# A final norm by token: rows turned first, squares summed along the row on ScalarE

## The chip, the cores and the metric

The kernel runs on one core of a Trainium2 chip. The metric is the device time of one execution in microseconds (us), the median of several runs. Engines: TensorE (PE) multiplies matrices, VectorE (DVE) and ScalarE (ACT) work on tiles of 128 partitions, GpSimd (POOL) is nearly idle here, SyncE (SP) issues DMAs, and so does ACT.

## The reference

One decoder layer on 512 tokens of 1024 features, fp32: a SwiGLU FFN, a mixer, a second FFN, then a gated embedding and a final norm. The last two are what the change touches:

```
gate = jax.nn.sigmoid(rmsnorm(h, ple_norm[i]) @ ple_w_gate[i] + ple_b_gate[i])
h = h + gate * (p[i] @ ple_w_proj[i])
return rmsnorm(h, final_norm)

def rmsnorm(x, g):
    y = xf * lax.rsqrt(jnp.mean(xf * xf, axis=-1, keepdims=True) + EPS)
    return (y * g.astype(jnp.float32)).astype(x.dtype)
```

## The kernel before, in words

Activations lie feature by feature: h[0] to h[7] are tiles of 128 features (partitions) by 512 tokens. In the program's names h[0], h[1], h[2], h[3] are h_91, h_92, h_93, h_94, and h[4] to h[7] are h_97, h_95, h_96, h_98. A product with a weight tile is done in three passes of split numbers (whi, wlo by x), 8 times over: 24 matmuls into one PSUM bank (b). The kernel first records all its operations; then it issues them in the order of ORDER, a table of unit numbers written out by hand or by a planner, engine queues being filled in that order. Each engine then runs its own queue strictly in order.

The last stage starts where the weights of ple_gate come in: raw (loaded by SP), whi (a cast on ACT), wlo (a subtraction on DVE). The token factors of the norm before it come from column sums, a root by Newton steps on DVE, a spread matmul, and a copy to rall on ACT. Then for each of the 8 feature tiles gate() multiplies the product by rall on DVE, takes the sigmoid with the bias on ACT, multiplies by the embedding and adds to h on DVE. For d = 0 to 4 this is done for all 512 tokens at once; the last three (BY_HALF = 3) are done by halves of 256 tokens: first the three for the first half, then the three for the second.

The final norm of before works by feature up to the end. gate() squares the new h (ACT, the last tile on DVE), the squares of the first five tiles are added into one tile (total, in the trace ssum), gained() multiplies h by the norm's vector, feature by feature. factors() sums over the partitions with matmuls against a column of ones (128x1), in fp32, for two chunks of 128 tokens, and takes the root by ACT's Sqrt table (rsqrt_by_table). rows_out() then turns h (4 transposes of 128 x 128 make one bank of 128 tokens by 512 features), and an evacuation multiplies by the token's factor and writes o, which goes to DRAM. The turns of both halves stand behind the last product.

Of the kernel before, what the change touches and what calls it, by code (L numbers as in the profile page):

```python
# [29 lines left out]
P = 128  # L30
# [22 lines left out]
    "m": 33, "convin": 2, "o": 8, "sq": 4,  # L53
}
REGION = dict.fromkeys(("raw0", "s0", "embt", "F", "xfa", "xfb", "x", "xa", "xb", "r4", "u", "emb"), "left") | dict.fromkeys(
    ("rawb", "whix", "wlox", "s1", "rawd", "ghi", "glo", "g", "u2", "p7", "m", "convin", "o", "sq"), "right",
# [20 lines left out]
for _name, _w in _VECS:  # L77
# [211 lines left out]
def layer_kernel(ctx: ExitStack, tc: tile.TileContext, a: dict, out: bass.AP):  # L289
# [1508 lines left out]
    def gate(d, ps, tok, engine):  # L1798

        t = tmp()[:, tok]  # L1800
        nc.vector.tensor_tensor(t, ps[:, tok], r[:, tok], ALU.mult)
        nc.scalar.activation(t, t, AF.Sigmoid, bias=col("ple_b_gate", d))
        engine.tensor_tensor(t, t, emb[d][:, tok], ALU.mult)
        engine.tensor_tensor(h[d][:, tok], h[d][:, tok], t, ALU.add)
        sq = tmp() if tok is whole else sb("sq", (P, half))
        if d < ND - 1:
            nc.scalar.activation(sq, h[d][:, tok], AF.Square)
        else:
            nc.vector.tensor_tensor(sq, h[d][:, tok], h[d][:, tok], ALU.mult)
        return sq  # L1810

    def gained(d, tok):

        if d < ND - 1:
            nc.scalar.activation(h[d][:, tok], h[d][:, tok], AF.Copy, scale=col("final_norm", d))
        else:
            nc.vector.tensor_scalar(
                h[d][:, tok], h[d][:, tok], col("final_norm", d), None, ALU.mult
            )

    total = sb("ssum")

    def done(d, ps):
        sq = gate(d, ps, whole, nc.vector)
        if d == 0:
            nc.vector.tensor_copy(total, sq)
        else:
            nc.vector.tensor_tensor(total, total, sq, ALU.add)
        gained(d, whole)

    for d in range(ND - BY_HALF):
        ps = mm_ps()
        accumulate(ps, weights(a["ple_gate"][d], D), 0, x)
        if d == 0:
            tok, first = norm.per_token(D), ps
            continue
        if d == 1:
            r = Norm.on_all(tok)
            done(0, first)
        done(d, ps)  # L1840
    units = [weights(a["ple_gate"][d], D) for d in range(ND - BY_HALF, ND)]
    def gate_half(i, tok):
        d = ND - BY_HALF + i
        ps = sm_ps()
        accumulate(ps[:, tok], units[i], 0, x, tokens=tok)
        sq = gate(d, ps, tok, nc.vector)
        gained(d, tok)
        return sq

    def factors(tok, sqs):  # L1850

        chunks = range(tok.start // P, tok.stop // P)
        ps = sm_ps()
# [8 lines left out]
        return rt  # L1862

    def rows_out(tok, rt):
        for i, c in enumerate(range(tok.start // P, tok.stop // P)):
            for q in range(2):
                ps = mm_ps()
                for d in range(4):
# [144 lines left out]
```

## Time and profile before

| | |
|---|---|
| median of 3 runs | 1074.15 us (1074.07 to 1074.2) |
| the profiled execution | 1073.36 us |
| its span, from first to last instruction | 1071.6 us |
| busy: PE, DVE, ACT, POOL | 99%, 76%, 52%, 7% of the span |
| granted TensorE clock | 0.999 of full |
| DMA | 173.27 MB, mean 162 GB/s |

Times in the rows are us from the span's start, durations us unless marked ns. A row of the timeline that stands for several instructions gives the time from the first's start to the last's end. PEld is the loading of the stationary tile, beside PE. A queue's name with a q (SPq, ACTq) is the issue of DMAs.

### The profile page before, as it was taken

The numbers are of one execution on the slowest core, as the hardware profiler recorded it, in microseconds if no ns is written. First come the engines' busy times: TensorE is split into PE (matmuls) and PEld (weight loads), VectorE is DVE, ScalarE is ACT, GpSimd is POOL, SyncE is SP. The second block draws the span as 40 slices with busy tenths as digits, with TensorE's granted clock in tenths as the row PEclk, the third lists the DMA queues.
The fourth block names the chain that finished last, engine by engine and source line by source line (L and its number), as shares of the span: only waits on it lengthen the run. The fifth ranks groups of instructions, "written<-read, shape, count | busy, mean of one in ns | idle before, by whom it ended". The sixth has DMA issues, their size and how long they took to land.

```text
span 1071.6 us, 17611 instructions
## 1 busy us (share of the span) xinstructions
PE 1062.1 (99%) x7151; PEld 965.0 (90%) x7151; DVE 817.0 (76%) x1169; ACT 559.5 (52%) x781; POOL 75.2 (7%) x95
## 2 busy tenths in 40 slices
PE   9999999999999999999999999999999999999997
PEld 7899999999998878998999888999999999999887
DVE  6978685867577879999999767988667575857866
ACT  7655344444444537887865435654434343534545
POOL 1100000100000000000100000010100000000000
PEclk9999999999999999999999999999999999999999
DMA  9876765766452236777855435786755757633412
GB/s 322 238 202 166 196 181 193 196 181 174 99 154 82 65 113 146 187 201 175 212 135 130 138 98 137 218 236 186 204 143 155 211 144 197 181 115 85 139 53 79
DMA packets 52209, 173.27 MB, mean 162 GB/s; under 512 B 5920, under 2 KB 6176, under 8 KB 52128
## 3 DMA queue, kind: packets, MB, share of 16 engines
q1 hardware_dynamic: 33696, 116.93, 32.1%
q0 software_dynamic: 12256, 44.57, 23.1%
q10 hardware_dynamic: 6176, 10.65, 3.4%
q8 instruction: 56, 0.92, 0.3%
q14 instruction: 25, 0.20, 0.1%
HBM read 167.86 MB, written 4.26 MB: 161 GB/s over the span
## 4 chain that ended last, share of the span: by engine, by line
PE 99%; DVE 0%; ACT 0%; issue 0%; DVEq 0%; ACTq 0%
PE b L1905 81%; PE a L1905 18%; DVEq L2008 0%; DVE o L1905 0%; ACT m L1905 0%; ACT b L1905 0%; DVE tmp L1905 0%; DVE h L1905 0%; DVE ones L410 0%; DVE nv L1905 0%; ACTq L1905 0%
## 5 line engine op out<-in xcount | busy, mean ns | idle before, releaser
L1905 PE MATMUL b<-xfb,whi 128*128 128x256 f32 (+1 forms) x1704 | 297.5, 278 | 0.7 <-ACT b L1905 0.7
L1905 PEld LDWEIGHTS b<-xfb,whi 128*128 128x128 f32 x1704 | 261.0, 188 | 6.0 <-ACT b L1905 0.9
L1905 PE MATMUL b<-xfb,wlo 128*128 128x256 f32 (+1 forms) x852 | 237.2, 278 | 0.0
L1905 ACT CAST whi<-raw 128x1024 fp32r<-128x1024 f32 (+1 forms) x131 | 136.0, 1041 | 146.4 <-PE b L1905 109.7
L1905 DVE TENSOR_TENSOR wlo<-raw,whi 128x1024 fp32r<-128x1024 f32 (+1 forms) x130 | 156.8, 1212 | 28.7 <-ACT whi L1905 25.8
L1905 PEld LDWEIGHTS b<-xfb,wlo 128*128 128x128 f32 x852 | 159.9, 188 | 0.5
L1905 PE MATMUL b<-xfa,whi 128*128 128x256 f32 (+1 forms) x696 | 124.0, 281 | 0.0
L1905 PEld LDWEIGHTS b<-xfa,whi 128*128 128x128 f32 x696 | 107.0, 188 | 2.5 <-DVE xfa L1905 0.2
L1905 PE MATMUL b<-xfa,wlo 128*128 128x256 f32 (+1 forms) x348 | 97.8, 281 | 0.0
L1905 ACT CAST whix<-rawd 128x1024 fp32r<-128x1024 f32 (+1 forms) x40 | 39.4, 986 | 88.5 <-PE a L1905 47.9
L1905 DVE TENSOR_TENSOR wlo<-rawb,whi 128x1024 fp32r<-128x1024 f32 x51 | 62.1, 1220 | 23.2 <-ACT whi L1905 23.1
L1905 ACT CAST whi<-rawb 128x1024 fp32r<-128x1024 f32 x51 | 53.3, 1049 | 48.8 <-PE b L1905 39.7
L1905 PE MATMUL b<-m,whi 128*128 128x512 f32 x224 | 69.6, 392 | 0.0
L1905 DVE TENSOR_TENSOR wlox<-rawd,whix 128x1024 fp32r<-128x1024 f32 (+1 forms) x40 | 45.7, 1143 | 27.0 <-ACT whix L1905 26.9
L1905 PEld LDWEIGHTS b<-xfa,wlo 128*128 128x128 f32 x348 | 65.4, 188 | 0.5
L1905 PE MATMUL b<-xb,whi 128*128 128x256 f32 (+1 forms) x280 | 62.2, 318 | 0.0
L1905 PE MATMUL b<-ghi,wlox 128*128 128x512 f32 x156 | 61.4, 394 | 0.0
L1905 PE MATMUL b<-glo,whix 128*128 128x512 f32 x156 | 61.2, 392 | 0.0
L1905 PE MATMUL b<-ghi,whix 128*128 128x512 f32 x156 | 60.7, 389 | 0.0
L1905 PE MATMUL a<-ghi,wlox 128*128 128x512 f32 x140 | 55.2, 394 | 0.0
L1905 PE MATMUL a<-glo,whix 128*128 128x512 f32 x140 | 54.9, 392 | 0.0
L1905 PE MATMUL a<-ghi,whix 128*128 128x512 f32 x140 | 54.4, 389 | 0.0
(294 smaller groups left out, 2223.8 us busy)
## 6 DMA issues: line engine op xcount, KB each, us to landing
raw<-in_ffn_gu SPq DMA_DIRECT2D x57, 512.0 KB, 5.4
rawd<-in_ffn_down SPq DMA_DIRECT2D x40, 512.0 KB, 4.4
raw<-in_ffn_gu POOLq DMA_DIRECT2D x32, 512.0 KB, 7.7
rawb<-in_ffn_gu SPq DMA_DIRECT2D x31, 512.0 KB, 6.1
s<-in_ffn_gu SPq DMA_DIRECT2D x21, 512.0 KB, 5.5
s<-in_ffn_gu POOLq DMA_DIRECT2D x21, 512.0 KB, 8.5
raw<-in_w_out SPq DMA_DIRECT2D x16, 512.0 KB, 3.6
raw<-in_w_in SPq DMA_DIRECT2D x13, 512.0 KB, 3.7
```

The lines of the kernel that those rows point to most:

```text
L1905: getattr(getattr(real, engine), what)(*(real_of(x) for x in args), **{k: real_of(x) for k, x in kw.items()})
```

## The change

The norm is done by token on turned rows. As soon as h is final for four feature tiles and two chunks of tokens, these are turned into PSUM, and ACT squares them there and sums along the row in the same instruction (accum_out), in three parts for each half: all of the first four feature tiles, then three of the others, then the last one. The norm's vector is loaded once, spread to all partitions (fn, 512 KB, issued on ACT's queue), and multiplied in on the turned rows: for the first half together with the token's factor in one DVE instruction; for the second half the upper four features are multiplied by fn early (upper()) and by the factor on ACT. The first half takes its root by Newton steps on DVE (rsqrt), the second by the Sqrt table, which a small ACTIVATE calls in ahead. The column sums, the squares by feature, their total and gained() go. ORDER was written anew for this; the sizes of the other tiles' places were kept.

```diff
-    "m": 33, "convin": 2, "o": 8, "sq": 4,
+    "m": 33, "convin": 2, "o": 8, "ssq": 10, "fn": 1, "t": 6, "junk": 2,
...
-    "1-2 5-7 9-10 13 12 11 3 14 16 18 20 24 15 17 19 0 25 21 77 26 41 27 29 42 38 37 39-40 34 8 35 43 33 "
+    "1-2 5 0 6-7 9-10 13 12 11 3 14 16 18 20 24 15 17 19 25 21 77 26 41 27 29 42 38 37 39-40 34 8 35 43 "
...
-        engine.tensor_tensor(t, t, emb[d][:, tok], ALU.mult)
-        engine.tensor_tensor(h[d][:, tok], h[d][:, tok], t, ALU.add)
-        sq = tmp() if tok is whole else sb("sq", (P, half))
...
+        nc.vector.tensor_tensor(t, t, emb[d][:, tok], ALU.mult)
+        nc.vector.tensor_tensor(h[d][:, tok], h[d][:, tok], t, ALU.add)
+
+    fn = sb("fn", (P, D))
+    nc.scalar.dma_start(fn, a["fn"].partition_broadcast(P))
...
+        def turn(self, q, part=slice(0, 4)):
+            for i, c in enumerate(self.chunks):
...
+                for d in range(part.start, part.stop):
+                    nc.tensor.transpose(chunk(ps, d), chunk(h[4 * q + d], c), ident)
+
+        def squares(self, q, part, n):
+            for i in range(2):
+                w = slice(part.start * P, part.stop * P)
+                nc.scalar.activation(
+                    sb("junk")[:, w], self.ps[q, i][:, w], AF.Square, accum_out=self.ss[n][:, i : i + 1]
+                )
+
+        def upper(self):
+            for i in range(2):
+                self.o[0, i] = sb("o")
+                nc.vector.tensor_tensor(self.o[0, i], self.ps[0, i], fn[:, :T], ALU.mult)
...
+            for i, c in enumerate(self.chunks):
+                rows = out[c * P : (c + 1) * P]
+                if self.half:
+                    o = self.o[0, i]
+                    nc.scalar.activation(o, o, AF.Copy, scale=rt[:, i : i + 1])
+                else:
+                    o = sb("o")
+                    nc.vector.scalar_tensor_tensor(
+                        o, self.ps[0, i], rt[:, i : i + 1], fn[:, :T], ALU.mult, ALU.mult
+                    )
+                (nc.scalar if self.half else nc.sync).dma_start(rows[:, :T], o)
+                o = sb("o")
+                nc.vector.scalar_tensor_tensor(o, self.ps[1, i], rt[:, i : i + 1], fn[:, T:], ALU.mult, ALU.mult)
+                nc.sync.dma_start(rows[:, T:], o)
...
+    rows = [Rows(i) for i in range(2)]
+    for row in rows:
+        row.turn(0)
+        row.squares(0, slice(0, 4), 0)
+        if row.half:
+            row.upper()
...
+    for tok, row in zip(halves, rows):
+        for i in range(BY_HALF - 1):
+            gate_half(i, tok)
+        row.turn(1, slice(0, 3))
+        row.squares(1, slice(0, 3), 1)
+        row.so_far()
+        gate_half(BY_HALF - 1, tok)
+        if row.half:
+            nc.scalar.activation(sb("ssq", (P, 2)), ones[:, 0:2], AF.Sqrt)
+        row.turn(1, slice(3, 4))
+        row.squares(1, slice(3, 4), 2)
+        row.out()
```

First place: PE's queue behind the last half product (of h_98, second half). Before, the column sums (ones) follow it, and then the first of 32 turns (ident), of which the rest stand behind these.

```order
L1905 MATMUL b_10793<-x_10224,wlo_10691 128x256
L1905 MATMUL b_10854<-ones_71,ssum_10670 128x1 x2
L1905 MATMUL b_10854<-ones_71,sq_10395 128x1 x2
L1905 MATMUL b_10854<-ones_71,sq_10397 128x1 x2
L1905 MATMUL b_10854<-ones_71,sq_10398 128x1 x2
L1905 MATMUL b_10878<-ident_65,h_91 128x128
L1905 MATMUL b_10878<-ident_65,h_92 128x128
L1905 MATMUL b_10878<-ident_65,h_94 128x128
L1905 MATMUL b_10878<-ident_65,h_93 128x128
```

In the changed kernel the same product (now b_10834) is followed by eight turns alone, which end PE's queue.

```order
L1928 MATMUL b_10834<-x_10230,wlo_10643 128x256
L1928 MATMUL b_10895<-ident_65,h_97 128x128
L1928 MATMUL b_10895<-ident_65,h_95 128x128
L1928 MATMUL b_10895<-ident_65,h_96 128x128
L1928 MATMUL b_10899<-ident_65,h_97 128x128
L1928 MATMUL b_10899<-ident_65,h_95 128x128
L1928 MATMUL b_10899<-ident_65,h_96 128x128
L1928 MATMUL b_10895<-ident_65,h_98 128x128
L1928 MATMUL b_10899<-ident_65,h_98 128x128
```

The other 24 turns moved ahead: 8 stand before the product b_10777, the last but one, and 16 (banks b_10814, b_10819, b_10824, b_10829) between it and b_10834.

Second place: ACT's queue at the same time. Before, sigmoids (tmp), squares by feature (sq) and multiplications by the norm's vector (h) stand in turn, and the table load for the root follows the last sigmoid.

```order
L1905 ACTIVATE sq_10397<-h_96 128x256
L1905 ACTIVATE tmp_10835<-tmp_10835,vec_63 128x256
L1905 ACTIVATE h_95<-h_95,vec_63 128x256
L1905 ACTIVATE h_96<-h_96,vec_63 128x256
L1905 ACTIVATE tmp_10852<-tmp_10852,vec_63 128x256
L1905 ACTIVATE h_93<-h_93,vec_63 128x512
L1905 ACT_TABLE_LOAD
L1905 ACTIVATE ny_10872<-nv_10866 128x2
```

Now squares of turned rows (junk, with the sum in ssq) stand there, and the sigmoid t_10892, of the last product, behind six of them.

```order
L1928 ACTIVATE junk_10862,ssq_10432<-b_10814 128x128
L1928 ACTIVATE t_10812<-t_10812,vec_63 128x256
L1928 ACTIVATE junk_10865,ssq_10433<-b_10814 128x384
L1928 ACTIVATE junk_10867,ssq_10433<-b_10824 128x384
L1928 ACTIVATE junk_10869,ssq_10432<-b_10824 128x128
L1928 ACTIVATE junk_10871,ssq_10434<-b_10829 128x512
L1928 ACTIVATE junk_10873,ssq_10434<-b_10819 128x512
L1928 ACTIVATE t_10892<-t_10892,vec_63 128x256
```

The squares by feature and the multiplications by the vector went; six squares of PSUM banks stand between the first of the 16 turns and the last sigmoid.

Third place: DVE's queue around the step that reads the last product. Before, it is tmp_10852, read from b_10793, with nothing but the last tile's own work ahead of it.

```order
L1905 TENSOR_TENSOR sq_10398<-h_98 128x256
L1905 TENSOR_SCALAR h_98<-h_98,vec_63 128x256
L1905 TENSOR_TENSOR tmp_10852<-b_10793,rall_10640 128x256
L1905 TENSOR_TENSOR tmp_10852<-tmp_10852,emb_10226 128x256
L1905 TENSOR_SCALAR nv_10866<-b_10854 128x2
L1905 TENSOR_TENSOR h_98<-h_98,tmp_10852 128x256
```

Now o_10443 (the norm's vector on a turned bank) and the first half's factor (nv, ny, nt) stand ahead of t_10892, which reads b_10834; in brackets what each row waits for.

```order
L1928 TENSOR_TENSOR o_10443<-b_10819,fn_10424 128x512 [waits DMAHW4_49,PE_49,Activation_49]
L1928 TENSOR_TENSOR t_10812<-t_10812,emb_10237 128x256
L1928 TENSOR_TENSOR ssq_10435<-ssq_10431,ssq_10433 128x2
L1928 TENSOR_TENSOR h_95<-h_95,t_10812 128x256 [waits DVE_49]
L1928 TENSOR_TENSOR ssq_10436<-ssq_10432,ssq_10435 128x2 [waits DVE_49]
L1928 TENSOR_SCALAR nv_10882<-ssq_10436 128x2 [waits DVE_49]
L1928 TENSOR_SCALAR ny_10884<-nv_10882 128x2 [waits DVE_49]
```

Five more small rows of the factor follow, and then t_10892. Behind it on DVE:

```order
L1928 TENSOR_TENSOR h_98<-h_98,t_10892 128x256
L1928 SCALAR_TENSOR_TENSOR o_10444<-b_10814,rlast_141,fn_10424 128x512
L1928 SCALAR_TENSOR_TENSOR o_10445<-b_10772,rlast_141,fn_10424 128x512
L1928 TENSOR_TENSOR ssq_10438<-ssq_10434,ssq_10437 128x2
L1928 SCALAR_TENSOR_TENSOR o_10446<-b_10824,rlast_141,fn_10424 128x512
L1928 TENSOR_SCALAR ssq_10438<-ssq_10438 128x2
L1928 SCALAR_TENSOR_TENSOR nv_10924<-ssq_10439,ssq_10438 128x2
L1928 SCALAR_TENSOR_TENSOR o_10447<-b_10767,rlast_141,fn_10424 128x512
```

Then come the second half's factor (rlast_142) and o_10448, o_10449, o_10450. ACT's last two rows multiply o_10443 and o_10450 by that factor and send them out.

## Rows read from the trace of the kernel before

**Rows 1.** The page: span, and busy time with its share by engine.
```profile
span 1071.6 us, 17611 instructions
PE 1062.1 (99%) x7151; PEld 965.0 (90%) x7151; DVE 817.0 (76%) x1169; ACT 559.5 (52%) x781; POOL 75.2 (7%) x95
```
**Rows 2.** Busy us by stretch: PE, PEld, DVE, ACT, POOL, clock, DMA share, GB/s.
```profile
1010.98:1057.37 46.39, 46.39 (x275) 41.06 (x274) 32.49 (x63) 23.36 (x37) 0.00 (x0) 1.00 0.16 51
...
1057.37:1066.53 9.16, 7.36 (x66) 6.88 (x64) 6.78 (x21) 6.16 (x11) 0.00 (x0) 1.00 0.32 117
```
**Rows 3.** The chain of waits from 1000: start, length, what.
```profile
1005.54 57.18 PE b L1905 x346
...
1065.87 0.66 DVE o L1905
```
**Rows 4.** Timeline of PE at the end: start, length, instruction, count.
```profile
1057.01 0.40 PE L1905 MATMUL b<-x,whi 128*128 128x256 f32 x2
...
1057.37 0.50 PE L1905 MATMUL b<-ones,ssum 128*128 128x1 f32 x4
...
1059.08 1.95 PE L1905 MATMUL b<-ident,h 128*128 128x128 f32 x16
1060.86 0.50 PE L1905 MATMUL b<-ones,ssum 128*128 128x1 f32 x4
...
1062.56 2.29 PE L1905 MATMUL b<-ident,h 128*128 128x128 f32 x16
```
**Rows 5.** Timeline of ACT, single rows from 1013 to the end.
```profile
1013.01 1.14 ACT L1905 ACTIVATE tmp<-h 128x512 f32<-128x512 f32 x2
...
1029.35 0.59 ACT L1905 COPY rall<-b 128x512 f32<-128x512 f32 x1
...
1040.71 0.62 ACT L1905 ACTIVATE tmp<-h 128x512 f32<-128x512 f32 x1
...
1049.39 0.91 ACT L1905 ACTIVATE tmp<-tmp,vec 128x256 f32<-128x256 f32 x2 [1.75 <-DVE tmp L1905]
...
1058.47 0.71 ACT L1905 ACTIVATE h<-h,vec 128x512 f32<-128x512 f32 x1
1059.19 1.28 ACT L1905 ACT_TABLE_LOAD   x1
1060.49 0.20 ACT L1905 ACTIVATE ny<-nv 128x2 f32<-128x2 f32 x1
1060.60 0.40 ACT L1905 ACTIVATE sq<-h 128x256 f32<-128x256 f32 x1
...
1064.19 1.27 ACT L1905 ACTIVATE o<-b,rlast 128x512 f32<-128x512 f32 x2 [0.48 <-PE b L1905]
```
**Rows 6.** Timeline of DVE, single rows from 1024 to the end.
```profile
1024.30 0.15 DVE L1905 TENSOR_TENSOR nt<-ny 128x4 f32<-128x4 f32 x1
1024.49 0.16 DVE L1905 SCALAR_TENSOR_TENSOR nt<-nt,nv 128x4 f32<-128x4 f32 x1
...
1030.53 1.88 DVE L1905 TENSOR_TENSOR tmp<-b,rall 128x512 f32<-128x512 f32 x3
...
1057.61 0.42 DVE L1905 TENSOR_TENSOR tmp<-b,rall 128x256 f32<-128x256 f32 x1
1058.60 0.43 DVE L1905 TENSOR_TENSOR tmp<-tmp,emb 128x256 f32<-128x256 f32 x1 [0.57 <-ACT tmp L1905]
...
1059.33 0.75 DVE L1905 TENSOR_TENSOR h<-h,tmp 128x256 f32<-128x256 f32 x2
...
1064.45 2.07 DVE L1905 TENSOR_SCALAR o<-b,rlast 128x512 f32<-128x512 f32 x3 [0.53 <-PE b L1905]
```
**Rows 7.** Output DMAs: SP's last, issued at 1066.9; ACT's of 1063.7.
```profile
L1905 SPq DMA_DIRECT2D out<-o x1: 677/677/677, 1066.9 to 1066.9; - x1
...
DMA to landing us min/median/max: 3.1/3.1/3.1
...
DMA to landing us min/median/max: 2.1/2.1/2.1
```

More of the change, by code (lines that the diff above doesn't have):

```diff
@@ L52 @@
     "whix": 1, "wlox": 1, "s1": 2, "rawd": 2, "ghi": 3, "glo": 3, "g": 1, "u2": 1, "p7": 1,
-    "m": 33, "convin": 2, "o": 8, "sq": 4,
+    "m": 33, "convin": 2, "o": 8, "ssq": 10, "fn": 1, "t": 6, "junk": 2,
 }
 REGION = dict.fromkeys(("raw0", "s0", "embt", "F", "xfa", "xfb", "x", "xa", "xb", "r4", "u", "emb"), "left") | dict.fromkeys(
-    ("rawb", "whix", "wlox", "s1", "rawd", "ghi", "glo", "g", "u2", "p7", "m", "convin", "o", "sq"), "right",
+    ("rawb", "whix", "wlox", "s1", "rawd", "ghi", "glo", "g", "u2", "p7", "m", "convin", "o", "fn", "t", "junk", "ssq"), "right",
 )
@@ L1796, in layer_kernel, with gate @@
     whole, halves = slice(0, T), (slice(0, half), slice(half, T))
-    def gate(d, ps, tok, engine):
-        t = tmp()[:, tok]
+    def gate(d, ps, tok):
+        t = sb("t")[:, tok]
         nc.vector.tensor_tensor(t, ps[:, tok], r[:, tok], ALU.mult)
         nc.scalar.activation(t, t, AF.Sigmoid, bias=col("ple_b_gate", d))
-        engine.tensor_tensor(t, t, emb[d][:, tok], ALU.mult)
-        engine.tensor_tensor(h[d][:, tok], h[d][:, tok], t, ALU.add)
-        sq = tmp() if tok is whole else sb("sq", (P, half))
[L1806 to L1829, printed above, removed]
+        nc.vector.tensor_tensor(t, t, emb[d][:, tok], ALU.mult)
@@ new lines, in gate, with __init__, so_far, out @@
+        nc.vector.tensor_tensor(h[d][:, tok], h[d][:, tok], t, ALU.add)
+    fn = sb("fn", (P, D))
+    nc.scalar.dma_start(fn, a["fn"].partition_broadcast(P))
+    class Rows:
+        def __init__(self, half):
+            self.half = half
+            self.chunks = range(half * (NC // 2), (half + 1) * (NC // 2))
+            self.ss = [sb("ssq", (P, 2)) for _ in range(3)]
+            self.ps, self.o = {}, {}
+        def turn(self, q, part=slice(0, 4)):
+            for i, c in enumerate(self.chunks):
+                if (q, i) not in self.ps:
+                    self.ps[q, i] = mm_ps()
+                ps = self.ps[q, i]
+                for d in range(part.start, part.stop):
[10 more added lines that the diff above has]
+                nc.vector.tensor_tensor(self.o[0, i], self.ps[0, i], fn[:, :T], ALU.mult)
+        def so_far(self):
+            self.e = sb("ssq", (P, 2))
+            nc.vector.tensor_tensor(self.e, self.ss[0], self.ss[1], ALU.add)
+            if self.half:
+                nc.vector.tensor_scalar(self.e, self.e, 1.0 / D, EPS, ALU.mult, ALU.add)
+        def out(self):
+            rt = sb("rlast", (P, 2))
+            if self.half:
+                v, y, t = (sb(n, (P, NC))[:, :2] for n in ("nv", "ny", "nt"))
+                nc.vector.scalar_tensor_tensor(v, self.ss[2], 1.0 / D, self.e, ALU.mult, ALU.add)
+                nc.scalar.activation(y, v, AF.Sqrt)
+                nc.vector.reciprocal(y, y)
+                nc.vector.tensor_tensor(t, y, y, ALU.mult)
+                nc.vector.scalar_tensor_tensor(t, t, -0.5, v, ALU.mult, ALU.mult)
+                nc.vector.scalar_tensor_tensor(rt, t, 1.5, y, ALU.add, ALU.mult)
+            else:
+                v = sb("ssq", (P, 2))
+                nc.vector.tensor_tensor(v, self.ss[2], self.e, ALU.add)
+                rsqrt(rt, v, 1.0 / D, (P, 2))
+            for i, c in enumerate(self.chunks):
+                rows = out[c * P : (c + 1) * P]
+                if self.half:
+                    o = self.o[0, i]
+                    nc.scalar.activation(o, o, AF.Copy, scale=rt[:, i : i + 1])
+                else:
+                    o = sb("o")
[6 more added lines that the diff above has]
+                nc.sync.dma_start(rows[:, T:], o)
@@ L1838, in layer_kernel @@
             r = Norm.on_all(tok)
-            done(0, first)
-        done(d, ps)
+            gate(0, first, whole)
+        gate(d, ps, whole)
     units = [weights(a["ple_gate"][d], D) for d in range(ND - BY_HALF, ND)]
+    rows = [Rows(i) for i in range(2)]
[4 more added lines that the diff above has]
+            row.upper()
     def gate_half(i, tok):
@@ L1845, in gate_half @@
         accumulate(ps[:, tok], units[i], 0, x, tokens=tok)
[L1846 to L1853, printed above, removed]
-        for j, sq in enumerate([total[:, tok]] + sqs):
-            for i in range(len(chunks)):
-                nc.tensor.matmul(
-                    ps[:, i : i + 1], sq[:, i * P : (i + 1) * P], ones[:, 0:1], start=i + j == 0,
-                    stop=j == len(sqs) and i == len(chunks) - 1, skip_group_check=True,
-                )
-        rt = sb("rlast", (P, 2))
-        rsqrt_by_table(rt, ps[:, :2], 1.0 / D, (P, 2))
[L1862 to L1868, printed above, removed]
-                    nc.tensor.transpose(chunk(ps, d), chunk(h[4 * q + d], c), ident)
-                o = sb("o")
-                if q == 0:
-                    nc.scalar.activation(o, ps, AF.Copy, scale=rt[:, i : i + 1])
-                else:
-                    nc.vector.tensor_scalar(o, ps, rt[:, i : i + 1], None, ALU.mult)
-                (nc.sync if q else nc.scalar).dma_start(out[c * P : (c + 1) * P, q * T : (q + 1) * T], o)
-    squares_of = [[], []]
-    for i in range(BY_HALF):
-        squares_of[0].append(gate_half(i, halves[0]))
-    for i in range(BY_HALF):
-        if i == BY_HALF - 1:
-            r_a = factors(halves[0], squares_of[0])
-        squares_of[1].append(gate_half(i, halves[1]))
-    rows_out(halves[0], r_a)
-    rows_out(halves[1], factors(halves[1], squares_of[1]))
+        gate(d, ps, tok)
+    for tok, row in zip(halves, rows):
[10 more added lines that the diff above has]
+        row.out()
     homes["psum"].open(psum)
@@ L1983, in _laid_out @@
     o["gm_w"] = np.ascontiguousarray(one["gm_w_s"].transpose(2, 0, 1).reshape(P, 8 * P))
+    o["fn"] = one["final_norm"].reshape(1, D)
     o["gm_b"] = one["gm_b_s"].reshape(1, 8 * P)
```

88 rows, old and new, of the table ORDER are left out of this document.

## The prediction

> **What bounds the kernel now.** I read the page first: the span is 1071.6 us and TensorE (PE) is busy for 99% of it [rows 1]. That share is an average, and the change touches only the last stage, so I asked for busy time in two stretches of it. From 1010.98 to 1057.37, the products of the last projection, PE is busy in all 46.39 us while VectorE (DVE) has 32.49 and ScalarE (ACT) 23.36. From 1057.37 to the last evacuation at 1066.53, 9.16 us, PE is busy 7.36 and DVE 6.78 [rows 2]. In the chain of waits PE holds the program in one piece up to 1062.7; from there DVE and PE take turns, and the last piece is an evacuation on DVE [rows 3]. So up to 1057.4 only PE's own work or a stall of PE counts; behind that, what counts is a dependence chain through PE, DVE and ACT.
>
> The tail of before, in PE's rows: the last product ends at 1057.37; column sums for the first half take 1.71 us (1057.37 to 1059.08), 16 turns 1.78, then column sums for the second half (1.70 to the next turn) and 16 more turns [rows 4]. Then three evacuations on DVE end at 1066.5 [rows 6], the last DMA is issued at 1066.9 and lands 3.1 later, at 1070.0 [rows 7]; the span ends 1.6 after that.
>
> **What the change removes, adds and moves.** On PE, 16 column sums go, all from the tail (1.71 + 1.70 = 3.41 us). The 32 turns stay, but 8 now stand before the last product but one and 16 before the last product. A turn costs 1.78/16 = 0.111 us [rows 4], so the last product ends 24 x 0.111 = 2.67 us later, at 1060.04, if PE does not stall before it. A half product is 24 matmuls at 0.12 (three from 1057.01 to 1057.37), 2.87 us, so the 16 turns end at 1057.17 and the first four of them at 1055.84.
>
> On ACT the squares of the stage by feature and the multiplications by the norm's vector go, and squares of turned rows come. They stand in the order shown: after the first four turns a square of 128, the sigmoid of t_10812, squares of 384, 384, 128, 512 and 512. A square of 512 takes a step of 0.52 (1.14 - 0.62), one of 256 takes 0.40 as a single row and so a step of 0.30 [rows 5]; by the two, 0.41 for 384 and 0.20 for 128. The sigmoid's step is 0.41. Together 0.20 + 0.41 + 2 x 0.41 + 0.20 + 2 x 0.52 = 2.67 us, begun at 1056.0: they end at 1058.7.
>
> These squares also sum along the row, which no instruction of the trace does. At the low end the sum comes with the pass and costs nothing. At the high end it is read out by an instruction like the smallest ACTIVATE, 0.20, and the 0.10 that two ACTIVATEs overlap is lost: 0.30. I take 0.21, the same lost 0.10 and the step of 0.11 that this smallest row has to the next (1060.49 to 1060.60) [rows 5]. Six such squares stand ahead of the next step, so it moves by 6 x 0.2 = 1.2 us, with ends 0 and 1.8.
>
> On DVE the next step is o_10443, which reads the bank of the last of these squares and by its row waits for ACT as well as for PE. It stands early in DVE's queue, ahead of the second half's gates, of the factor of the first half, and of t_10892, the first step behind the last product. I therefore start it at 1058.8 (without the sum's price). From there, in DVE's order: o_10443 0.60, a product and an addition of 256 at 0.34 each, a small addition 0.15: 1060.25. Eight dependent small instructions at 0.20 (1024.30 to 1024.49 is one step) follow: t_10892 starts at 1061.85, though its product ended at 1060.04 [rows 6]. Before, the same step started 0.24 behind its product (1057.61).
>
> From t_10892 to the product with the embedding took 0.99 us before (1057.61 to 1058.60, the sigmoid between). With 0.5 for that product and a small one, and 0.34 for the addition to h_98, that ends at 1063.68. Two turns and two squares of 128 follow beside DVE, which has four evacuations of the first half to do: o_10444, o_10445, a small one, o_10446, two small ones, o_10447, four small dependent ones of the second factor, o_10448, o_10449, o_10450. With 0.66 for an evacuation (2.07 for three, 0.75 the last [rows 6]) this is 6 x 0.66 + 0.60 + 0.15 + 0.35 + 0.80 = 5.86 us: 1069.54. The table load for the square root, 1.28, lies beside these evacuations; without them it would be late next. o_10450 then goes through ACT (0.1 and 0.69, as o<-b,rlast there) and out: 1070.33, against 1066.9 before. I let its DMA land in 2.4 us, between 2.1 of a lone one and 3.1 of before's last [rows 7], and add the same 1.6: 1074.3. With 1.2 for the row sums: 1075.5, which is 3.9 over 1071.6. The ends of the sum's price give 1074.3 and 1076.1.
>
> Where nothing is charged: the broadcast of the norm's vector is issued before the ACT table load, some 25 us ahead of its first reader, in a stretch in which the DMA engines move 51 GB/s on the mean [rows 2]. Two more output DMAs on SP and two fewer on ACT lie under DVE's evacuations. The eight embedding loads go to the queue closer together and earlier; their first reader stands behind the token factors. The reordering at the end of the second FFN moves splits and norms among the three engines, while PE keeps the same products; I charge nothing, since PE has its weights split several products ahead.
>
> The page "PSUM — Partial Sum Buffer" of the Trainium skill (section on bank collisions) speaks against this change: no two engines may be at the same bank at once, two reads included, and software must order them. The order of the changed kernel agrees, since o_10443 waits for ACT; no row of before has two engines read one bank, and without such a rule the sum would be the second rival's.
>
> **How this stands to the median.** The profiled execution took 1073.36 us, 1.76 over its span; the median of the runs is 1074.15. With 3.9 added: 1077.3 and 1078.0. What a measurement of this kernel can tell from no change is 0.2%, 2.1 us.
>
> **Rivals.**
> First, not slower: DVE keeps pace, and the 3.41 us of column sums come back. This holds if the first half's factor and evacuations are done by 1060.0, when the last product ends. Then gate 1.75, turn and two squares 0.9, table load and root 1.5, factor 0.8, two multiplications on ACT 1.3, which gives 1066.3 for the last issue instead of 1066.9, about 0.7 less: 1073.4. For it: the sums are gone. Against it: four evacuations stand behind h_98 in DVE's order, so they can't be done by then. It decides if DVE has under 3 us of work left at 1063.7; I count 5.9. Chance 0.07.
>
> Second, the change does less than I say: o_10443 does not wait for the squares in effect. DVE then does it at 1056.7, and t_10892 starts with its product's end, 1060.1. The whole tail comes 1.7 earlier and the price of the sums, 1.2, is hidden: 1072.6 for the span, 1.0 over before, 1075.2 for the median. Chance 0.10.
>
> Third, PE stalls before the last products. ACT copied the token factors (rall) at 1029.35 and DVE used them from 1030.53 [rows 5, 6]. Now the copy stands behind a cast whose buffer the fourth full product frees, at about 1034.7, and the sigmoids behind one that the fifth frees, at about 1040.1; everything by DVE comes some 6 us later. By the same durations the last piece of h that the 16 turns need is there at 1054.5, and PE wants it at 1055.4. If ACT and DVE are 2 us later than that, PE stalls 1.1: 1079.1. For it: the thin margin. Against: in this stretch DVE was busy for 70% alone. Chance 0.13.
>
> Fourth, the table load costs more. In the trace the load of 1.28 begins 0.01 after the ACTIVATE before it and the next begins 0.02 after its end [rows 5]. If a switch took twice that row, 2.56, behind squares that end at 1064.5, the root would be there at 1067.3 where DVE wants it at 1066.8 (both 1.2 later with the sums): about 0.5 more, 1078.5. The Trainium skill's page "ScalarE: Activation LUTs" (section What ACT_TABLE_LOAD costs) has it so: about 1.28 us for the load and 1.38 for a drain. The row agrees with the first and shows nothing of the second. Chance 0.05.
>
> **How the numbers follow.** The forecast, with its own ends (1076.8 to 1078.7 for the median), has 0.65. The range goes down to the second rival and up past the third: 1075.0 to 1079.6; below it lie the first rival and a little of the second, above it a long stall or a dearer row sum. Slower by over 0.2% is all of the forecast but about 0.05 of it at a cheap sum, the third and the fourth: 0.77. Within 0.2%: the second rival, that 0.05 and most of the first: 0.20. Faster by more: 0.03.
>
> **What would show it.** Right: a last product that ends near 1060.0 without idle time of PE before it; o_10443 on DVE idle until the last of the six squares; t_10892 1.5 us or more behind its product; DVE nearly without gaps from o_10443 to o_10450; the last issue on ACT's queue. Wrong: DVE idle for over 1 us behind 1061, o_10443 begun before the squares end, PE idle before the last product, or squares whose step exceeds 0.52 by 0.3 or by nothing.

## The result and the profile after

| | before | after |
|---|---|---|
| median | 1074.11 us (1073.48 to 1074.72, 14 runs) | 1076.41 us (1075.56 to 1077.24, 14 runs) |
| the profiled execution | 1073.36 us | 1076.27 us |
| its span | 1071.6 us | 1074.6 us |

The ratio is 1.0026, 95% interval 1.0019 to 1.0033: slower by 2.3 us in the medians. Span against span it is 3.0 us, because the profiled execution of before lay 0.75 under its median and that of after 0.14 under.

The page of after, span and busy time by engine [rows 1]:

```profile
span 1074.6 us, 17552 instructions
PE 1059.2 (99%) x7119; PEld 961.0 (89%) x7119; DVE 815.9 (76%) x1174; ACT 555.3 (52%) x785; POOL 75.2 (7%) x95
```

PE has 2.9 us less to do and DVE 1.1 less, and the span is 3.0 longer. So it is a matter of order, in the last stage. The two stretches of [rows 2], cut anew at the end of the last product (1060.06) and of the last evacuation on DVE (1070.23):

```profile
1010.98:1060.06 49.08, 49.08 (x301) 43.70 (x299) 30.30 (x58) 19.25 (x37) 0.00 (x0) 1.00 0.14 44
1060.06:1070.23 10.17, 1.96 (x10) 0.92 (x8) 9.05 (x32) 4.38 (x13) 0.00 (x0) 0.67 0.37 134
```

Up to the last product PE is busy without a gap, with the granted clock at full. The 0.67 behind it is a mean: full clock (2.4 GHz) up to 1063, the lower level (1.2 GHz) from 1064 on; in the three microseconds from 1060 PE had worked for 0.54, 0.28 and 0.37 us. It is not what costs: the last two turns took 0.66 us in this run and 0.44 in its repetition (below), where the clock fell later, and the two ends, counted from the same turn, are 0.04 apart. Behind the last product the parts have changed: before, PE was busy for 7.36 of 9.16 us; now DVE is, for 9.05 of 10.17. PE's rows at the end [rows 4]; in brackets the idle time ahead and its releaser:

```profile
1055.45 1.91 PE L1928 MATMUL b<-ident,h 128*128 128x128 f32 x16
...
1060.06 0.32 PE L1928 MATMUL b<-ident,h 128*128 128x128 f32 x1
1060.84 0.44 PE L1928 MATMUL b<-ident,h 128*128 128x128 f32 x2 [0.46 <-DVE h L1928]
1062.63 0.55 PE L1928 MATMUL b<-ident,h 128*128 128x128 f32 x3 [1.35 <-DVE t L1928]
1064.18 0.66 PE L1928 MATMUL b<-ident,h 128*128 128x128 f32 x2 [1.00 <-ACT junk L1928]
```

The last product ends at 1060.06, 2.69 later than before, and from there PE waits. ACT in the same stretch [rows 5]:

```profile
1056.14 0.28 ACT L1928 ACTIVATE junk<-b 128x128 f32<-128x128 f32 x1 [1.70 <-PE b L1928]
1056.32 0.20 ACT L1928 ACTIVATION_READ_ACCUMULATOR junk<-b 128x1 f32 x1
1056.41 0.50 ACT L1928 ACTIVATE t<-t,vec 128x256 f32<-128x256 f32 x1
...
1058.56 0.62 ACT L1928 ACTIVATE junk<-b 128x512 f32<-128x512 f32 x1
1059.04 0.24 ACT L1928 ACTIVATION_READ_ACCUMULATOR junk<-b 128x1 f32 x1
1062.61 0.51 ACT L1928 ACTIVATE t<-t,vec 128x256 f32<-128x256 f32 x1 [3.34 <-DVE t L1928]
...
1065.30 1.28 ACT L1928 ACT_TABLE_LOAD   x1
1066.60 0.20 ACT L1928 ACTIVATE ssq<-ones 128x2 f32<-128x2 f32 x1
...
1070.26 0.72 ACT L1928 ACTIVATE o<-o,rlast 128x512 f32<-128x512 f32 x1 [1.75 <-DVE o L1928]
```

Each square is followed by a row of its own that reads the sum out. The six squares (and one sigmoid) run from 1056.14 to 1059.28; then ACT stands idle for 3.34 us, for DVE. And DVE [rows 6]:

```profile
1056.44 0.42 DVE L1928 TENSOR_TENSOR h<-h,t 128x256 f32<-128x256 f32 x1
1059.31 0.69 DVE L1928 TENSOR_TENSOR o<-b,fn 128x512 f32<-128x512 f32 x1 [2.44 <-ACT junk L1928]
...
1062.16 0.42 DVE L1928 TENSOR_TENSOR t<-b,rall 128x256 f32<-128x256 f32 x1
...
1063.95 1.40 DVE L1928 SCALAR_TENSOR_TENSOR o<-b,rlast,fn 128x512 f32<-128x512 f32 x2
...
1067.59 0.16 DVE L1928 SCALAR_TENSOR_TENSOR rlast<-nt,ny 128x2 f32<-128x2 f32 x1
1068.22 1.41 DVE L1928 SCALAR_TENSOR_TENSOR o<-b,rlast,fn 128x512 f32<-128x512 f32 x2 [0.47 <-DVE rlast L1928]
1069.55 0.68 DVE L1928 TENSOR_TENSOR o<-b,fn 128x512 f32<-128x512 f32 x1
```

This is the reading on which everything rests: DVE idles 2.44 us ahead of o_10443 for ACT's last square, at a time when PE is still busy with the last product; and t<-b,rall, the first step behind that product, starts 2.10 us after it (1062.16 against 1060.06). Before, it was 0.24. The idle time and the time that the path loses are in different places of DVE's queue. The last output is issued on ACT's queue and lands 2.0 later; the span ends 1.6 after that, as before [rows 7]:

```profile
L1928 ACTq DMA_DIRECT2D out<-o x1: 344/344/344, 1071.0 to 1071.0; - x1
...
DMA to landing us min/median/max: 2.0/2.0/2.0
```

### The profile page after: what moved, and what is told of

It is laid out like the page before. It is cut to its first block, busy times and chain, and to the rows that moved or that the text cites. A ratio compares the mean times of both kernels' runs of the same rounds, so it can differ in the third digit from the quotient of the medians.

```text
span 1074.6 us, 17552 instructions
## 1 busy us (share of the span) xinstructions
PE 1059.2 (99%) x7119; PEld 961.0 (89%) x7119; DVE 815.9 (76%) x1174; ACT 555.3 (52%) x785; POOL 75.2 (7%) x95
## 4 chain that ended last, share of the span: by engine, by line
PE 97%; DVE 1%; ACT 1%; DMA 0%; issue 0%; SPq 0%; DVEq 0%; ACTq 0%
PE b L1928 80%; PE a L1928 18%; DVE o L1928 0%; DMA g<-in_p 0%; ACT junk L1928 0%; DVE t L1928 0%; DVE nt L1928 0%; ACT t L1928 0%; SPq L1928 0%; DVE h L1928 0%; ACT o L1928 0%; DVE glo L1928 0%; DVEq L2032 0%; ACT ghi L1928 0%; ACT m L1928 0%
```

## The experiments

A measure that holds for all variants: the time from the first of the 16 turns to the end of the span, the tail. The runs reach that turn at times up to 1.2 us apart (1054.79 to 1056.03), with the same work ahead of it (0.66 between the change and its repetition, which are one program), and the tail leaves that out. After has 1074.6 - 1055.45 = 19.15. Before ended the product ahead of that point at 1057.37 - 2.87 = 1054.50; the 8 turns that now stand earlier would have made it 0.89 later, 1055.39, so its tail is 1071.6 - 1055.39 = 16.2. Each ratio is to executions of before taken with that run; their medians lie between 1072.98 and 1074.11.

| run | first of the 16 turns | tail us | span us | median us | ratio to before, 95% |
|---|---|---|---|---|---|
| the change | 1055.45 | 19.15 | 1074.6 | 1076.41 | 1.0026 (1.0019 to 1.0033) |
| the change again | 1054.79 | 19.11 | 1073.9 | 1076.74 | 1.0025 (1.0015 to 1.0036) |
| o_10443 later | 1055.98 | 17.12 | 1073.1 | 1074.41 | 1.0009 (1.0000 to 1.0018) |
| its square first | 1055.46 | 17.04 | 1072.5 | 1074.20 | 1.0004 (0.9995 to 1.0013) |
| 16 turns behind | 1056.00 | 22.0 | 1078.0 | 1079.55 | 1.0054 (1.0039 to 1.0069) |
| before, fewer sums | - | - | 1071.5 | 1073.26 | 0.9998 (0.9989 to 1.0006) |
| no row sums | 1056.03 | 18.27 | 1074.3 | 1076.13 (one run) | - |
| another order | 1054.93 | 17.47 | 1072.4 | 1074.19 | 1.0012 (1.0003 to 1.0021) |
| factor on GpSimd | 1054.99 | 17.51 | 1072.5 | 1074.75 | 1.0015 (1.0006 to 1.0023) |
| two Newton steps | 1055.68 | 16.92 | 1072.6 | 1074.37 | 1.0009 (0.9999 to 1.0018) |

In "16 turns behind" the turns no longer mark that point; it is taken as the end of the same product, 0.20 ahead of DVE's t<-b,rall for it (1056.20), as in after.

**The wait taken off the path.** In the table of the order unit 2644 is o_10443, 2706 the t<-b,rall of the last product.

```diff
-... 2697-2698 2644 2692 2659 2693 2669-2676 2706 2677 2699-2700 ...
+... 2697-2698 2692 2659 2693 2669-2676 2706 2677 2644 2699-2700 ...
```

> The changed kernel with one DVE instruction moved: the multiplication of the turned bank by the norm's vector (o_10443), which idles 2.44 us for ScalarE's last square of that bank, stands behind the first step of the last gate instead of ahead of it, beside the sigmoid. Theory (the wait delays everything behind it on DVE): t<-b,rall of the last product starts within 0.2 us of the product's end at 1060.06 instead of 2.10 behind it; o_10443's 0.6 stays on the path, so the last addition to h and all evacuations come about 1.5 us earlier, span 1073.1, median about 1074.9 against 1076.4. Rival A (the last product itself is late by the 24 turns, and that is what costs): DVE idles somewhere else, the span stays within 0.4 of 1074.6. Rival B (DVE's amount of work from the last product on sets the end): the idle time goes, but so does nothing else; again within 0.4 of 1074.6.

DVE's timeline of this run; the row t<-b,rall now waits for PE:

```profile
1060.79 0.42 DVE L1928 TENSOR_TENSOR t<-b,rall 128x256 f32<-128x256 f32 x1 [0.41 <-PE b L1928]
...
1061.20 0.68 DVE L1928 TENSOR_TENSOR o<-b,fn 128x512 f32<-128x512 f32 x1
...
1062.86 1.40 DVE L1928 SCALAR_TENSOR_TENSOR o<-b,rlast,fn 128x512 f32<-128x512 f32 x2
```

The row starts 0.20 behind its product (1060.59, which is 4.61 behind the first turn, as in the change). Neither rival fits. That the span, 1073.1, is the theory's to the digit is luck: the tail is 2.0 shorter where 1.5 was forecast, and this execution reached the first turn 0.5 later. Of the 2.0, some 0.4 is not the wait: DVE stood idle 0.47 behind rlast in the change and 0.11 here (more on it below).

**The same by ACT's order.** Unit 2642 is the square of o_10443's bank; DVE's and PE's queues keep their order.

```diff
-... 2696 2668 2691 2658 2657 2667 2641-2642 2697-2698 ...
+... 2696 2668 2691 2642 2658 2657 2667 2641 2697-2698 ...
```

> The changed kernel with one ScalarE instruction moved: the square of the bank that o_10443 reads comes first of the four large squares instead of last; PE's and DVE's queues stay as they are. Theory: o_10443 starts at about 1057.5 instead of 1059.31, the small steps of the first half's factor follow its sums at 1058.7, and t<-b,rall of the last product starts at its end, 1060.1, instead of 1062.16: everything behind comes 1.6 to 2.0 us earlier, span 1072.6 to 1073.0, median about 1074.5. Rival A (the turns ahead of the last product are the cost) and rival B (amount of work on DVE): span within 0.4 of 1074.6, since neither is changed. If one bank could be read by both engines without an order, this would also change nothing.

DVE's timeline:

```profile
1057.54 0.69 DVE L1928 TENSOR_TENSOR o<-b,fn 128x512 f32<-128x512 f32 x1 [0.66 <-ACT junk L1928]
...
1060.40 0.42 DVE L1928 TENSOR_TENSOR t<-b,rall 128x256 f32<-128x256 f32 x1
...
1065.83 0.16 DVE L1928 SCALAR_TENSOR_TENSOR rlast<-nt,ny 128x2 f32<-128x2 f32 x1
1066.10 1.41 DVE L1928 SCALAR_TENSOR_TENSOR o<-b,rlast,fn 128x512 f32<-128x512 f32 x2
```

The wait fell from 2.44 to 0.66, t<-b,rall starts 1.76 earlier, and the tail is 2.1 shorter: with one ACT instruction moved, nothing is left that this measurement could tell from the kernel before. The prediction's second rival (o_10443 does not wait in effect) gave 1072.6 for the span; here it has been made true, and the span is 1072.5 (with a landing of 2.0 instead of the 2.4 that was charged). Of the 2.1, 0.36 is again the gap behind rlast, 0.11 here; the other 1.75 is the wait, more than half of the 2.95 by which the tail had grown.

**The turns moved back.**

```diff
-... 2690 2666 2656 2640 2665 2655 2639 2705 2637-2638 ...
+... 2690 2705 2666 2656 2640 2665 2655 2639 2637-2638 ...
```

> The changed kernel with the 16 turns of the first half's last tile and the second half's first bank moved behind the last product on PE; nothing else moves. The last product then ends at 1058.28 instead of 1060.06. Rival A (a late last product is the cost): 1.8 us faster, span 1072.8. Theory (DVE's wait on the squares, which wait on the turns, is the cost): the squares start 2.87 later, o_10443 and all behind it on DVE too, and the earlier product helps nothing: span about 1077.4, 2.8 us slower, median about 1079.2.

PE's first turn behind the last product, then DVE's rows:

```profile
1058.88 1.91 PE L1928 MATMUL b<-ident,h 128*128 128x128 f32 x16
...
1062.72 0.69 DVE L1928 TENSOR_TENSOR o<-b,fn 128x512 f32<-128x512 f32 x1 [5.31 <-ACT junk L1928]
...
1065.58 0.42 DVE L1928 TENSOR_TENSOR t<-b,rall 128x256 f32<-128x256 f32 x1
```

The last product ended at 1058.88, by the tail's point 1.7 us earlier (2.88 behind it instead of 4.61), and the kernel is 2.85 slower by the tail: a product takes 2.87. In the changed kernel the last product is not what the end hangs on; the turns, through squares and o_10443, are.

**What the column sums had cost.** In the kernel before, only the last tile's sums are kept.

```diff
-                nc.tensor.matmul(
-                    ps[:, i : i + 1], sq[:, i * P : (i + 1) * P], ones[:, 0:1], start=i + j == 0,
...
+                if j == len(sqs):
+                    nc.tensor.matmul(
+                        ps[:, i : i + 1], sq[:, i * P : (i + 1) * P], ones[:, 0:1], start=i == 0,
```

> The kernel before, with 6 of the 8 column-sum matmuls of each half left out (the sums of the total and of two tiles are missing in the factor): it asks what the removal of column sums alone is worth. PE loses 12 matmuls of 0.21, 2.56 us, all behind the last product. Rival (PE's tail was the bound, so what it loses is gained): 2.5 us faster, span 1069.1. Theory (what stands beside them on ScalarE and DVE, the table load that ends at 1060.47, the first factor and the multiplications by the norm's vector, takes their place): 0.3 to 0.8 us faster, span 1070.8 to 1071.3, and the rows of the first factor stay where they are (reciprocal near 1060.7).

PE's timeline of this run, from the first sums to the last turns:

```profile
1057.53 0.60 PE L1906 MATMUL b<-ones,sq 128*128 128x1 f32 x4
1057.99 0.53 PE L1906 MATMUL b<-ident,h 128*128 128x128 f32 x3
1059.39 1.64 PE L1906 MATMUL b<-ident,h 128*128 128x128 f32 x13 [0.88 <-ACT h L1906]
...
1062.89 1.64 PE L1906 MATMUL b<-ident,h 128*128 128x128 f32 x13 [0.80 <-DVE h L1906]
```

PE was given 2.56 us and stands idle for 1.68 of it, 0.88 for ACT and 0.80 for DVE, which multiply h by the norm's vector. The span fell by 0.1, or by 0.26 against the last product, which ended 0.16 later here; by this the theory's 0.3 to 0.8 was still a little too much (the medians, 0.35 apart with an interval from 1.2 faster to 0.6 slower, can't tell). So three quarters of the sums that the change removes, 2.56 of 3.41 us, were worth about 0.3 by the profile as long as the rest of the stage stayed: [rows 3] has PE in the chain there in one piece, but what lay beside it was only just hidden.

**The price of the row sums.**

```diff
-                    sb("junk")[:, w], self.ps[q, i][:, w], AF.Square, accum_out=self.ss[n][:, i : i + 1]
+                nc.scalar.activation(sb("junk")[:, w], self.ps[q, i][:, w], AF.Square)
...
-            self.ss = [sb("ssq", (P, 2)) for _ in range(3)]
+            self.ss = [ones[:, 0:2]] * 3
```

> The changed kernel with the squares made without the sum along the row: accum_out is left out and the factors are worked out from a constant instead, so the output misses the true sums. It prices the row sums on the path. In the changed kernel the six squares ahead of o_10443 run from 1056.14 to 1059.28. Theory (a row sum costs what the steps show, about 0.05 a square, since its read-out fills the overlap that two squares would have): the same six run some 0.3 to 0.4 us shorter, 0.52 a step for 512 and 0.41 for 384, o_10443 starts about 0.35 us earlier against the turns ahead of it, and the small steps of the first half's factor, which then wait for no sum, may start earlier too, but stand behind o_10443 in DVE's queue and gain only that 0.35. Rival (the forecast's price, 0.2 a square): 1.2 us shorter, o_10443 at about 1058.1.

ACT's timeline, then DVE's row:

```profile
1056.72 0.28 ACT L1926 ACTIVATE junk<-b 128x128 f32<-128x128 f32 x1 [1.88 <-PE b L1926]
1056.90 0.50 ACT L1926 ACTIVATE t<-t,vec 128x256 f32<-128x256 f32 x1
1057.30 2.01 ACT L1926 ACTIVATE junk<-b 128x384 f32<-128x384 f32 x5
```

```profile
1059.34 0.69 DVE L1926 TENSOR_TENSOR o<-b,fn 128x512 f32<-128x512 f32 x1 [1.90 <-ACT junk L1926]
```

The same seven instructions take 2.59 us (1056.72 to 1059.31) instead of 3.14, and DVE waits 1.90 instead of 2.44. Six row sums cost 0.55, or 0.09 each: between the two expectations, nearer to the first. The read-out row shows 0.20, but about half of it lies where two squares would overlap anyway. The tail is 0.88 shorter, since this run has not the gap behind rlast either.

**Another order, and less work for DVE.** The first moves units only. In the second the first half's factor runs on GpSimd, and SyncE issues all outputs.

```diff
-... 2641-2642 2697-2698 2644 2692 2659 2693 2669-2676 2706 2677 2699-2700 2707 2701-2702 2678-2679 2708 2680 2709 ...
-... 2685 2688 2682 2684 2686 2717-2720 2727 2723 2643 2725-2726 2721 2728 2724 2722
+... 2641 2697-2698 2692 2693 2644 2659 2669-2676 2706 2677-2679 2699-2700 2707 2701-2702 2710 2680 2708 2709 ...
+... 2715 2716 2685 2686 2643 2717-2720 2721 2725 2722 2726 2727-2728 2723-2724
```

> The changed kernel, same instructions, with the last stage in another order: the square of o_10443's bank first (as before in this study), the sqrt table's load ahead of the last squares, the other bank of the second half multiplied by the norm's vector before the second factor instead of at the very end, so that ScalarE's two last multiplications run beside DVE's last two evacuations. Theory (the tail is now bound by DVE's own work, 10.6 us from o_10443 on, which no order can shorten; only ScalarE's 0.7 behind DVE's last instruction can be hidden): DVE ends at about the same 1068, the last issue falls from 1068.9 to 1068.2, span 1071.7 to 1072.0, median 1073.5, no difference to the kernel before. Rival (the dependence chain through the second factor bounds, DVE's work does not): the earlier table load brings 0.6 more, span about 1071.1.

```diff
-                nc.vector.tensor_tensor(v, self.ss[2], self.e, ALU.add)
-                rsqrt(rt, v, 1.0 / D, (P, 2))
+                nc.gpsimd.tensor_tensor(v, self.ss[2], self.e, ALU.add)
...
+                for i in range(3):
+                    nc.gpsimd.tensor_tensor(t, y, y, ALU.mult)
+                    nc.gpsimd.tensor_tensor(t, t, w, ALU.mult)
...
-                (nc.scalar if self.half else nc.sync).dma_start(rows[:, :T], o)
+                nc.sync.dma_start(rows[:, :T], o)
```

> The same order, with the first half's factor (its sum, root and Newton steps, 15 small instructions instead of DVE's 11 because each Newton step takes four) on GpSimd, which is idle there, and all output DMAs issued by SyncE. DVE's queue behind o_10443 gets about 2.0 us shorter. Theory (DVE's work bounds the tail): if GpSimd takes no more than 0.2 a step, the factor is there at about 1061.8 and DVE ends 0.9 to 1.2 us earlier than in the order alone, last issue near 1067.4, span 1070.7 to 1071.0, median about 1072.7, which would be faster than the kernel before. If a step takes 0.3 or more, the factor comes at 1063.2 or later, DVE idles for it behind the last gate, and nothing is gained: span 1071.8 or more. Rival (DVE's work is not the bound): no difference to the order alone in either case.

In the first, DVE is done at 1067.37 and the last issue is at 1067.4, 1.0 us earlier by the tail than with the square first; 0.7 was forecast. The end did not follow: the tail is 0.4 longer, and the median is 0.12% over before's where no difference was forecast. The outputs come closer together and land later. Landing of SyncE's last two outputs in this order, then with the square first:

```profile
L1928 SPq DMA_DIRECT2D out<-o x2: 332/332/332, 1066.7 to 1067.4; - x2
...
DMA to landing us min/median/max: 2.7/3.1/3.4
```

```profile
L1928 SPq DMA_DIRECT2D out<-o x2: 332/332/333, 1066.9 to 1067.5; - x2
...
DMA to landing us min/median/max: 2.7/2.7/2.7
```

So theory and rival both fell short: the second half's 1 MB takes 4.1 to 4.2 us in both, from its first issue (ACT's queue, 1066.6 and 1066.8) to its last landing (1067.4 + 3.4 = 1070.8; with the square first ACT's last output, 1068.9 + 2.0 = 1070.9). On GpSimd most small steps took 0.27 to 0.28 against 0.20 on DVE, two took 0.53 and 0.47, and the factor came at 1062.84; DVE stood idle for it behind the last gate. GpSimd's first and last step, and DVE's row:

```profile
1058.34 0.20 POOL L1935 TENSOR_TENSOR ssq<-ssq,ssq 128x2 f32<-128x2 f32 x1 [94.75 <-ACT junk L1935]
...
1062.65 0.19 POOL L1935 TENSOR_TENSOR rlast<-nt,ny 128x2 f32<-128x2 f32 x1
```

```profile
1062.88 1.41 DVE L1935 SCALAR_TENSOR_TENSOR o<-b,rlast,fn 128x512 f32<-128x512 f32 x2 [1.19 <-POOL rlast L1935]
```

A step lies between the expectation's two branches, and nothing is gained, as in the second. But the rival had the same end, and the run changes two things, which don't act alike. DVE is done 0.7 later by the tail than in the order alone, and the last issue comes 1.3 later (1068.8). Against that, the last output lands 2.7 behind its issue instead of 3.4, and the span ends 1.0 behind that landing (1071.5 to 1072.5); in the other runs it ends 1.5 to 1.6 behind it. The last output's issue and landing:

```profile
L1935 SPq DMA_DIRECT2D out<-o x1: 399/399/399, 1068.8 to 1068.8; - x1
...
DMA to landing us min/median/max: 2.7/2.7/2.7
```

So this run does not settle what DVE's work is worth, and all outputs on SyncE with the factor left on DVE was not tried.

**The change again, and an earlier first half.** The second has the order above with two Newton steps, one evacuation of the first half ahead of t<-t,emb and one behind h_98; of its edit only the call of the root is shown.

```diff
-                rsqrt(rt, v, 1.0 / D, (P, 2))
+                rsqrt(rt, v, 1.0 / D, (P, 2), 2)
```

> The changed kernel once more, as it is. It asks two things: how far its start and its end move from one execution to another (over the runs so far the first turn that the wait hangs on began at 1054.9, 1055.5 or 1056.0, with the same instructions ahead of it), and whether the 0.47 us in which DVE stood idle between the second half's factor (rlast) and its next evacuation belongs to the program or to one execution. If it belongs to the program, the gap is there again; if not, this profile has 0.05 to 0.1 there, as the runs with one moved instruction have. Median 1076 to 1077, ratio to the kernel before between 1.0019 and 1.0033.

DVE's timeline of the repeated run:

```profile
1066.92 0.16 DVE L1928 SCALAR_TENSOR_TENSOR rlast<-nt,ny 128x2 f32<-128x2 f32 x1
1067.55 1.41 DVE L1928 SCALAR_TENSOR_TENSOR o<-b,rlast,fn 128x512 f32<-128x512 f32 x2 [0.47 <-DVE rlast L1928]
```

The gap is there again, to a hundredth: it belongs to the program. The tail, 19.11, agrees with 19.15, while the span differs by 0.7.

> The last stage in the better order, with two Newton steps instead of three for the first half's factor (slightly less exact), and with the first half's evacuations started in the shadow of the last sigmoid, so that the outputs begin about 1.5 us earlier. Theory (with the wait gone, DVE's chain of factor and evacuations and the streaming of 2.1 MB of outputs at about 380 GB/s bound the tail together): last issue about 0.8 us earlier than in the order alone, and fewer bytes still to stream then; counted from the first of the 16 turns, the span's end falls from 17.5 us to 16.5 us, which is 0.3 more than the kernel before would have by the same count (16.2); ratio to before between 1.0000 and 1.0010. Rival (what bounds is the last product and the chain behind it through sigmoid, squares and table load, which this leaves alone): 17.3 to 17.5 us as before.

The tail is 16.92, half-way between theory and rival. The last issue comes no earlier (1068.10, 12.4 behind the first turn, as in the other order), where 0.8 was forecast; only the crowding of the outputs is relieved (its landing takes 3.0 instead of 3.4). None of the versions tried beats the kernel before.

## Why the prediction was right, and which terms were not

**PE** (right). Last product at 1060.04 forecast, 1060.06 measured, without idle time. That the two agree to 0.02 is luck, since the same product ended at 1059.40 in the repetition; what holds is the price of the turns, 2.67 forecast and 2.61 measured (8.35 us from the first of the 24, at 1051.71, to the end of the last product, less two products of 2.87). The reordering earlier in the program cost nothing that shows, and the third rival's stall did not come.

**The wait** (right). o_10443 waits for the last square of its bank; forecast 1.8 to 3.0 for the delay of t<-b,rall behind its product, measured 2.10. Two experiments shortened the wait or took it off the path, by different means, and some 1.7 us of the loss went with it; a third made it longer by 2.87 and the kernel 2.85 slower. On the page "PSUM — Partial Sum Buffer" (section on bank collisions) the Trainium skill has it that software must order two reads of one bank: 2.44 us is how long DVE stands idle for that order here; no run shows what two engines at one bank would do without it.

**The row sums** (mis-sized, the largest error). I took 0.21 a square, 1.2 in all; they cost 0.09, 0.55 in all. I had added the lost overlap to a whole small step; only a part of the read-out comes on top. This is -0.65 of the forecast.

**Gate and DVE's queue** (right in sum). From t<-b,rall to the first evacuation 1.79 (1062.16 to 1063.95) against 1.83; beyond the row sums, t<-b,rall came 0.24 earlier than forecast, 0.20 of it behind the start of o_10443 (2.85 to it against 3.05). The queue took 6.28 against 5.86, all of it the 0.47 behind rlast, which nothing in [rows 6] announced.

**Landing** (mis-sized). 2.4 taken, 2.0 measured: the last output was issued 1.3 behind the one ahead of it (1069.7), before's only 0.4 (1066.5), so [rows 7] should have been read at its lower value. Together: -0.65 - 0.24 - 0.04 + 0.42 - 0.4 = -0.9, and 3.9 - 0.9 is the 3.0 between the spans. The two errors of size point the same way, and that the unforeseen gap hides 0.4 of their 1.05 is luck. The median, 1076.41, lies in the stated range but 0.4 below the forecast's own ends (1076.8 to 1078.7). In the medians the change costs 2.3, 0.7 less than between the spans; that is how the two profiled executions happened to lie.

**The rivals.** The first lived on the removed sums; DVE had 5.8 us of work left behind the last gate, and leaving out three quarters of the sums brought about 0.3. The fourth: the load took 1.28 and the next row began 0.02 after it, as in [rows 5]. The drain that the Trainium skill's page "ScalarE: Activation LUTs" (section What ACT_TABLE_LOAD costs) adds does not show here either.

What is left: the gap of 0.47 on DVE between rlast and the evacuation. It is in the change, in its repetition and in the run with the turns moved back, in which DVE's and ACT's queues stand in the same order, and in none of the other six of the changed kernel, in which an order or what DVE waits for is another. The chain of waits counts 0.41 of it as time in which DVE waits for nothing that the profile shows; what makes it was not tried. And of the 2.95 by which the tail grew, 1.75 is the wait and 0.36 this gap; the other 0.84 is still there with the square first (17.04 against 16.2), and no run takes it apart.

## What to carry to other kernels

In a queue that runs strictly in order, ask of each instruction that waits what is queued behind it and when that could have started; here a wait that ended while the busiest engine still worked on the last product cost some 1.7 us behind that product. Taking work from the engine at 99% was worth only the distance to the next chain beside it; leave the work out once and measure that distance before rebuilding. And where the bytes leave at the end, look at what lands: an earlier last issue that only crowded the outputs brought nothing here.

## What the runs showed of the hardware

A sum along the row on ScalarE appears as an instruction of its own, ACTIVATION_READ_ACCUMULATOR, 0.19 to 0.24 us long, but lengthens a series of squares by 0.09 each (3.14 against 2.59 us for six, one profile without the sums). A dependent 128x2 step is 0.20 us on VectorE and mostly 0.27 to 0.28 on GpSimd, from start to start. From the second half's factor (the end of rlast) to the end of the span 6.4 to 6.6 us passed in four orders of the tail (o_10443 later, its square first, the other order, two Newton steps); in that time 1 MB of outputs is made and sent, 4.1 to 4.2 us from the first issue to the last landing. With all outputs on SyncE it was 5.9, since the span ended 1.0 instead of 1.5 to 1.6 behind the last landing; why is open.
